# S5 coefficient generators moved from GpSimd to VectorE, and one sum and one scan per group pair in the S5 mixer

## The chip, the core and the metric

The kernel runs on one core of one Trainium2 chip. The metric is the device time of one execution in microseconds (us). In the text and in the profile the engines are PE (TensorE matmul), PEld (TensorE weight load), DVE (VectorE), ACT (ScalarE), POOL (GpSimd) and SP (SyncE, which here only issues DMAs). All data are fp32; large matmuls run on fp32r halves (a rounded high part and the rest), three matmuls for each product.

## What is computed

A network of two layers on 1024 latent tokens and 256 context tokens of width 1024. Layer 0 mixes with attention and retention, layer 1 with an S5 state space model; each is followed by an MLP of width 4096 with squared ReLU. The change touches the S5 part, whose coefficients depend on the inputs and are made on the chip:

```python
def s5_discretize(a_re, a_im, b_re, b_im, c_re, c_im, log_dt):
    a = lax.complex(f(a_re), f(a_im))
    dt = jnp.exp(f(log_dt))[:, None]
    a_bar = jnp.exp(dt * a)
    b_bar = ((a_bar - 1) / a)[..., None] * lax.complex(f(b_re), f(b_im))
    c_mat = lax.complex(f(c_re), f(c_im))
...
    # per step, 64 groups of 64 states and 16 channels, both directions
    bu = jnp.einsum('btgh,gph->btgp', u_blk.astype(jnp.complex64), b_bar)
    bu = bu.at[:, 0].add(a_bar * x)
    _, xs = lax.associative_scan(_affine_compose, (a, bu), axis=1)
    y = jnp.einsum('btgp,ghp->btgh', xs, c_mat).real
...
    z = jax.nn.gelu(y).astype(dtype) @ w_glu
    za, zb = jnp.split(z, 2, axis=-1)
    return za * jax.nn.sigmoid(zb)
```

## The kernel before

The program is written in a tile framework that allocates buffers, sets all semaphores, and orders the instructions of each engine by its own planning, in which code position is a priority; the order on an engine can therefore differ from the order in the code. Once built, each engine's queue and each DMA queue runs strictly in order.

**Layer 0's MLP** (`mlp`, called twice in `run`) first handles tokens 0 to 511 and the context, then tokens 512 to 1023. Sixteen rounds each make 256 hidden columns (`first`) and multiply the round before by the second matrix (`second`). Each 512 KB weight tile `mraw` is loaded on SP's queue and split by `split` into `uh`/`ul` or `dh`/`dl` (L76 on ACT, L84 on DVE); the hidden activations are made by a ReLU (L1053) and squares on ACT and a subtraction `al` on POOL (L84); results are added to `x` by DVE (L1070), which frees the PSUM bank.

**Under this MLP runs a generator of side work** (`side` in `run`). `beat` advances it by one step for every 1/RA (first call) or 1/RB (second call) matmuls of 512 columns. Its steps are the modulation of layer 1 (`ada_rest`), then `s5_gen`: `s5_base` (discretisation and powers of the poles; `pb`, `bb`), `s5_outputs` (the coefficients `oc` of the output side, stored to `cst`, with the lag matrices `s5_lags`), `s5_inputs` (the coefficients `wo` of the input side, 16 parts of two halves, stored to `bst` by ACT's queue) and `s5_tables` (sines and cosines, stored to `csd`), and at last layer 1's first normalisation (`s5_in`). `later(n, f)` puts `f` off by `n` steps. Complex products are made as two products and a sum; before the change most products run on POOL and the sums on DVE.

**The mixer** (`s5_main`) works on 32 pairs of groups. `load(q)` fetches the coefficients `B`, `C`, `Tt` and the table `CS` (three buffers), `spread(q)` completes `CS` on ACT. `states(q)` multiplies the inputs `ut` (L1503), rotates by `CS` (L1511), adds (L1512), scans along 160 columns with the decay `R8` (L1516, one scan for each direction and part) and rotates back to `sy` (L1519, two of three on POOL). `outs(q)` multiplies by `C` (L1537), and every fourth pair a GELU writes `Y`. In the code, `outs(q - 2)` follows `states(q)`.

**The GLU** (`glu`) transposes `Y`, splits it into `yh` and `yl`, and for each half of the tokens runs eight output columns of two 24-matmul products; `next(side, None)` advances a second generator, 24 steps of modulation for layer 1's MLP, each of four loads `aw` and four reductions (L216). Then comes layer 1's MLP.

`atile` hands out 32 shared tiles of 512 columns (and 16 of 256) to most of these parts.

Of the kernel before, what the change touches and what calls it, by code (L numbers as in the profile page):

```python
# [9 lines left out]
F32 = mybir.dt.float32  # L10
# [14 lines left out]
MAGIC = 12582912.0  # L25
NW = 14
RA = 0.07
RB = 0.125
BLOCKS = ((0, 512), (512, 512), (1024, 256))


# [20 lines left out]
class Net:  # L52
# [1091 lines left out]
    def s5_base(self):  # L1144
# [120 lines left out]
        for d in range(2):  # L1265
            o, w = self.atile(name="pb"), self.atile(name="pbw")
            o4, w4 = (x.rearrange("p (s r q) -> p s r q", s=8, r=2) for x in (o, w))
            e = slice(0, 8) if d == 0 else slice(7, None, -1)
            bc = lambda K: K[:, d::2].unsqueeze(1).to_broadcast([P, 8, 32])
            for r in range(2):  # L1270
                tt(o4[:, :, r], pr[:, e, d::2], bc((kr, ki)[r]), ALU.mult)
                nc.gpsimd.tensor_tensor(w4[:, :, r], pi[:, e, d::2], bc((ki, kr)[r]), ALU.mult)

            def add(o4=o4, w4=w4):
                tt(o4[:, :, 0], o4[:, :, 0], w4[:, :, 0], ALU.subtract)
                tt(o4[:, :, 1], o4[:, :, 1], w4[:, :, 1], ALU.add)
            self.later(1, add)

            def turn(d=d, o=o):
                tp = self.bank()  # L1280
                for k4 in range(4):
                    nc.tensor.transpose(tp[:, k4 * P:(k4 + 1) * P], o[:, k4 * P:(k4 + 1) * P], self.ident)
                st = self.atile(name="pbs")
                nc.scalar.activation(st, tp, AF.Copy)
                nc.sync.dma_start(bass.AP(tensor=self.pbd.tensor, offset=self.pbd.offset + d * 65536,
                                          ap=[[P, P], [16384, 4], [1, P]]), st.rearrange("j (k n) -> j k n", k=4))
            self.later(20, turn)
            yield

        for d in range(2):  # L1290
            x, o, t = ([self.atile(name=nm) for _ in range(2)] for nm in ("b", "bb", "bt"))
            self.bb += [o]
            for r in range(2):
                nc.scalar.dma_start(x[r], I["s5b"][r, :, d])
            kb = lambda K: K[:, d::2].unsqueeze(2).to_broadcast([P, 32, 16])
            g3 = lambda x: x.rearrange("p (g h) -> p g h", h=16)
            for r in range(2):
                tt(g3(o[r]), g3(x[r]), kb(kr), ALU.mult)
                nc.gpsimd.tensor_tensor(g3(t[r]), g3(x[1 - r]), kb(ki), ALU.mult)

            def add(d=d, o=o, t=t):
                tt(o[0], o[0], t[0], ALU.subtract)
                tt(o[1], o[1], t[1], ALU.add)
                for r in range(2):
                    v.tensor_copy(self.bx[:, d, r, 0:16], o[r][:, 496:512])
            self.later(1, add)
            yield

    def s5_tables(self):

# [31 lines left out]
    def s5_inputs(self):  # L1342

        nc, I = self.nc, self.I
        parts = [(d, g0) for d in range(2) for g0 in range(0, 64, 8)]

        def fetch(d, g0):
            b, w = ([self.atile(name=nm) for _ in range(2)] for nm in ("wb", "ww"))
            for r in range(2):
                nc.sync.dma_start(b[r], bass.AP(  # L1350
                    tensor=I["s5bt"].tensor, offset=I["s5bt"].offset + (d * 2 + r) * 4096 + g0 * 64,
                    ap=[[0, 8], [16384, 16], [1, 512]]))
                nc.sync.dma_start(w[r], bass.AP(
                    tensor=self.pbd.tensor, offset=self.pbd.offset + (d * 16 + r) * 4096 + g0 * 64,
                    ap=[[8192, 8], [0, 16], [1, 512]]))
            return b, w
        gpv = lambda x: x.rearrange("p (q n) -> p q n", n=P)
        nx = fetch(*parts[0])
        for _ in range(4):
            yield  # L1360
        for k, (d, g0) in enumerate(parts):
            b, w = nx
            if k + 1 < len(parts):
                nx = fetch(*parts[k + 1])
            qs = slice(g0 // 2, g0 // 2 + 4)
            for r in range(2):
                x, t = (self.atile(name="wo") for _ in range(2))
                nc.gpsimd.tensor_tensor(x, w[0], b[r], ALU.mult)
                yield
                nc.gpsimd.tensor_tensor(t, w[1], b[1 - r], ALU.mult)  # L1370
                self.later(2, lambda r=r, x=x, t=t: nc.vector.tensor_tensor(
                    x, x, t, ALU.add if r else ALU.subtract))
                self.later(5, lambda qs=qs, d=d, r=r, x=x: nc.scalar.dma_start(self.bst[:, qs, d, r], gpv(x)))
                yield
                yield

    def s5_outputs(self, gp):
# [6 lines left out]
        for it in range(16):  # L1384
# [6 lines left out]
            for d in range(2):  # L1391
# [6 lines left out]
                xb = [a.unsqueeze(2).to_broadcast([P, 2, 9, 16]) for a in x]  # L1398
                v9 = lambda t: t[:, :288].rearrange("p (q k h) -> p q k h", q=2, k=9)
                a, b, e, f = (self.atile(name="oc") for _ in range(4))  # L1400
                gp_tt = nc.gpsimd.tensor_tensor
                gp_tt(v9(a), xb[0], w[0], ALU.mult)
                gp_tt(v9(b), xb[1], w[1], ALU.mult)
                gp_tt(v9(e), xb[0], w[1], ALU.mult)
                gp_tt(v9(f), xb[1], w[0], ALU.mult)

                def join(a=a, b=b, e=e, f=f):
                    v.tensor_tensor(a[:, :288], a[:, :288], b[:, :288], ALU.subtract)
                    v.scalar_tensor_tensor(e[:, :288], e[:, :288], -1.0, f[:, :288], op0=ALU.mult, op1=ALU.subtract)
                self.later(2, join)  # L1410

                def store(qs=qs, d=d, a=a, e=e, k0=k0):
                    for r, t in enumerate((a, e)):
                        nc.scalar.dma_start(self.cst[:, qs, d, r], t[:, :288].rearrange("p (q k) -> p q k", q=2)[
                            :, :, 16 * k0:16 * k0 + P])
                self.later(5, store)
                o1[d] = [t[:, :288].rearrange("p (q k) -> p q k", q=2) for t in (a, e)]
                yield
            self.later(6, lambda it=it, o1=o1: self.s5_lags(it, o1))
            yield  # L1420

    def s5_lags(self, it, o1):
# [41 lines left out]
    def s5_main(self, p, last):  # L1464
# [1 line left out]
        nc = self.nc  # L1466
        v, gp, mm = nc.vector, nc.gpsimd, nc.tensor.matmul

        def inputs(g0, n):

            for s in range(8):
                nc.sync.dma_start(ut[112 - 16 * s:128 - 16 * s, g0:g0 + n],
                                  self.ud[16 * g0:16 * (g0 + n), s].rearrange("(g q) c -> q g c", q=16))
        self.Y = {(kt, th): self.atile(name="y") for kt in range(KT) for th in range(2)}
        sl, A, ybank = {}, {}, {}
# [18 lines left out]
            nc.scalar.activation(CS[:, :, 1], CS[:, :, 2], AF.Copy)  # L1494

        def states(q):
            B, C, Tt, CS = sl[q]
            for d in range(2):
                vb = self.bank()
                for r in range(2):  # L1500
                    for k in range(2):
                        u = ut[:, 2 * q + k, 0:160] if d == 0 else ut[:, 2 * q + k, 32:192]
                        mm(vb[64 * k:64 * k + 64, 160 * r:160 * r + 160], B[:, d, r, 64 * k:64 * k + 64], u,  # L1503
                           start=True, stop=True)
                t = p.tile([P, 640], F32, tag="st", name="st", bufs=2)
                t4 = t.rearrange("p (r w c) -> p r w c", r=2, w=2)
                vv = vb[:, 0:320].rearrange("p (r c) -> p r c", r=2)
                if d == 1:
                    vv = vv[:, :, ::-1]
                cs = CS[:, d].rearrange("p (r w) c -> p r w c", r=2)  # L1510
                v.tensor_tensor(t4, vv.unsqueeze(2).to_broadcast([P, 2, 2, 160]), cs[:, ::-1], ALU.mult)  # L1511
                v.tensor_tensor(t[:, 0:320], t[:, 0:320], t[:, 320:640], ALU.add)  # L1512
                z = p.tile([P, 320], F32, tag="sz", name="sz", bufs=3).rearrange("p (r c) -> p r c", r=2)
                a8 = self.R8[:, 2 * q + d:2 * q + d + 1].to_broadcast([P, 160])
                for r in range(2):
                    v.tensor_tensor_scan(z[:, r], a8, t[:, 160 * r:160 * r + 160], 0.0, ALU.mult, ALU.add)  # L1516
                y = p.tile([P, 512], F32, tag="sy", name="sy", bufs=6).rearrange("p (r w c) -> p r w c", r=2, w=2)
                e = gp if (2 * q + d) % 3 else v
                e.tensor_tensor(y if d == 0 else y[:, :, :, ::-1],  # L1519
                                z[:, :, 31:159].unsqueeze(2).to_broadcast([P, 2, 2, P]), cs[:, :, ::-1, 31:159],  # L1520
                                ALU.mult)
                A[q, d] = y

# [21 lines left out]
        for q in range(3):  # L1545
            load(q)
        ut = p.tile([P, 64, 192], F32, name="ut")
        for _ in range(3):
            next(last)
        inputs(0, 8)  # L1550
        self.drain(last)
        for q in range(32):
            spread(q)
# [10 lines left out]
    def glu(self, p, x, after, side):  # L1564
# [3 lines left out]
        for th in range(2):  # L1568
# [9 lines left out]
            for oc in range(KT):  # L1578
                b = []
                for w in (oc + KT, oc):  # L1580
                    wt = self.split(p, I["glu"][w], "u")
                    z = self.bank()
                    for kt in range(KT):
                        self.mm3(z, wt(kt), yT[kt], kt == 0, kt == KT - 1)
                        if kt % 4 == 3:
                            next(side, None)
                    b.append(z)
                sgm = p.tile([P, 512], F32, tag="r", name="sgm", bufs=2)
# [271 lines left out]
```

## Time and profile before

| what | us |
|---|---|
| median of three runs | 3227.12 (3220.26 to 3232.1) |
| the profiled execution | 3215.43 |
| its span, first to last instruction | 3213.6 |
| layer 0's MLP with the side work, in the profile | 1075 to 2081 |
| the mixer's loop over pairs, in the profile | 2102 to 2284 |

The profile is that of one execution. The page gives each engine's busy time over the whole span; a table of stretches gives the same for any part of it, with the TensorE clock that was granted (1.00 is full speed) and the share of time that the 16 DMA engines were busy. A list of waits says for how long an engine stood before a line and what ended it; a view by tile gives least, median and longest duration of each operation on that tile; a view by time lists instructions with start and duration, and in brackets the idle time before.

### The profile page before, as it was taken

The page shows a single profiled execution, that of the slowest core. Times are in us where ns is not written, and L with a number is a line of the kernel's source. Part 1 is how long each engine was busy: PE and PEld are TensorE (multiplying, and loading weights), DVE is VectorE, ACT ScalarE, POOL GpSimd, SP SyncE. Part 2 cuts the span into 40 slices and gives each one's busy share as a digit, 9 for nine tenths or more (in the row PEclk, how much of TensorE's full clock was granted, in tenths as well). Part 3 has the DMA queues.
Part 4 walks back from the last instruction along what each step waited for, and adds up shares of the span by engine and source line. Part 5 has one row for each costly group of instructions (what it writes and reads, how often), then busy time and mean ns, then how long its engine had stood idle before and what let it go on. Part 6 is the DMA issues. An engine that isn't in the chain of part 4 may idle for free. (4 is left out here: it accounts for less than half of the span.)

```text
span 3213.6 us, 45368 instructions
## 1 busy us (share of the span) xinstructions
PE 2968.0 (92%) x16683; PEld 2436.2 (76%) x16683; DVE 2111.0 (66%) x4014; ACT 1221.5 (38%) x2493; POOL 929.7 (29%) x902
## 2 busy tenths in 40 slices
PE   5899998899999998999997999967799999999998
PEld 3777777678878787887785778756678788888887
DVE  6777777687754688556468974378865555555555
ACT  6542222666762332222233664321334322222221
POOL 3642222455540113466326110123222111111111
PEclk8999999999999999999998999979999999999999
DMA  7132222301021452245426555287742111111111
GB/s 250 69 119 84 76 79 63 84 26 25 13 85 34 136 162 89 87 120 154 131 85 206 172 163 145 85 180 196 231 139 89 56 46 53 53 46 47 46 46 66
DMA packets 259039, 324.28 MB, mean 101 GB/s; under 512 B 72336, under 2 KB 179632, under 8 KB 258816
## 3 DMA queue, kind: packets, MB, share of 16 engines
q1 hardware_dynamic: 198352, 281.03, 29.0%
q10 hardware_dynamic: 59264, 36.84, 3.7%
q0 software_dynamic: 1200, 3.51, 0.4%
q8 instruction: 131, 2.15, 0.3%
q14 instruction: 92, 0.75, 0.1%
HBM read 267.96 MB, written 53.35 MB: 100 GB/s over the span
## 5 line engine op out<-in xcount | busy, mean ns | idle before, releaser
L84 POOL TENSOR_TENSOR al<-r,ah 128x512 fp32r<-128x512 f32 (+1 forms) x160 | 204.3, 1289 | 1191.5 <-ACT r L1057 1116.7
L1070 DVE SCALAR_TENSOR_TENSOR x<-b,mods,x 128x512 f32<-128x512 f32 (+1 forms) x483 | 457.5, 967 | 101.1 <-PE b L72 95.1
L84 DVE TENSOR_TENSOR ul<-mraw,uh 128x512 fp32r<-128x512 f32 x256 | 204.6, 803 | 429.3 <-ACT uh L76 428.7
L70 PE MATMUL b<-ah,dh 128*128 128x512 f32 (+1 forms) x1088 | 416.1, 383 | 21.4 <-ACT r L1053 10.2
L71 PE MATMUL b<-al,dh 128*128 128x512 f32 (+1 forms) x1088 | 413.7, 380 | 0.7 <-POOL al L84 0.7
L72 PE MATMUL b<-ah,dl 128*128 128x512 f32 (+1 forms) x1088 | 412.7, 380 | 0.5 <-DVE dl L84 0.4
L76 ACT ACTIVATE uh<-mraw 128x512 fp32r<-128x512 f32 x256 | 160.3, 628 | 453.3 <-PE b L71 261.3
L70 PE MATMUL b<-h2h,uh 128*128 128x512 f32 (+1 forms) x768 | 280.7, 366 | 21.8 <-DVE x L1070 11.6
L72 PE MATMUL b<-h2h,ul 128*128 128x512 f32 (+1 forms) x768 | 278.9, 364 | 18.6 <-DVE ul L84 18.4
L71 PE MATMUL b<-h2l,uh 128*128 128x512 f32 (+1 forms) x768 | 277.5, 361 | 0.0
L70 PEld LDWEIGHTS b<-ah,dh 128*128 128x128 f32 x1088 | 206.7, 190 | 64.8 <-DVE x L1070 11.6
L72 PEld LDWEIGHTS b<-ah,dl 128*128 128x128 f32 x1088 | 206.5, 190 | 40.5 <-DVE dl L84 1.9
L71 PEld LDWEIGHTS b<-al,dh 128*128 128x128 f32 x1088 | 207.0, 190 | 38.1 <-POOL al L84 1.1
L76 ACT ACTIVATE dh<-mraw 128x512 fp32r<-128x512 f32 x192 | 117.5, 627 | 248.2 <-PE b L71 119.6
L84 POOL TENSOR_TENSOR pl<-pe,ph 128x512 fp32r<-128x512 f32 (+1 forms) x128 | 158.3, 1246 | 154.9 <-ACT ph L76 86.8
L70 PE MATMUL b<-h3h,uh 128*128 128x512 f32 x512 | 202.0, 395 | 0.0
L71 PE MATMUL b<-h3l,uh 128*128 128x512 f32 x512 | 200.0, 391 | 2.0 <-DVE h3l L313 1.8
L72 PE MATMUL b<-h3h,ul 128*128 128x512 f32 x512 | 200.9, 393 | 0.0
L70 PEld LDWEIGHTS b<-h2h,uh 128*128 128x128 f32 x768 | 146.6, 191 | 50.5 <-DVE x L1070 14.2
L84 DVE TENSOR_TENSOR dl<-mraw,dh 128x512 fp32r<-128x512 f32 x192 | 150.5, 794 | 48.5 <-ACT dh L76 28.9
L72 PEld LDWEIGHTS b<-h2h,ul 128*128 128x128 f32 x768 | 146.4, 191 | 47.1 <-DVE ul L84 23.7
L1053 ACT ACTIVATE r<-b 128x512 f32<-128x512 f32 (+1 forms) x160 | 87.9, 550 | 244.9 <-PE b L72 170.8
(421 smaller groups left out, 7171.3 us busy)
## 6 DMA issues: line engine op xcount, KB each, us to landing
mraw<-in_w SPq DMA_DIRECT2D x192, 512.0 KB
aw<-in_adat SPq DMA_DIRECT2D x112, 256.0 KB
mraw<-in_glu SPq DMA_DIRECT2D x32, 512.0 KB
aw<-in_adat SPq DMA_DIRECT2D x96, 128.0 KB
CS<-csd SPq DMA_DIRECT2D x32, 320.0 KB
w<-in_adaw SPq DMA_DIRECT2D x32, 256.0 KB
wraw<-in_winr SPq DMA_DIRECT2D x32, 256.0 KB
cst<-oc ACTq DMA_DIRECT2D x64, 128.0 KB
```

The costliest lines, as they stand in the source:

```text
L70: mm(o, s[0], m[0], start=start, stop=False)
L71: mm(o, s[0], m[1], start=False, stop=False)
L72: mm(o, s[1], m[0], start=False, stop=stop)
L76: self.nc.scalar.activation(o, x, AF.Copy)
L84: e.tensor_tensor(o, x, h.bitcast(F32), ALU.subtract)
L1053: nc.scalar.activation(r[:, :n], b[:, :n], AF.Relu)
L1070: nc.vector.scalar_tensor_tensor(o, as_x(b), self.M[:, l, 5, oc, s:s + 1], xs, op0=ALU.mult, op1=ALU.add)
```

## The change

RB goes from 0.125 to 0.14. In `s5_base`, `s5_outputs` and `s5_inputs` all products move to DVE, each sum follows its products at once instead of one or two steps later, and `s5_base` and `s5_outputs` are divided into more steps (22 and 32 more). In `states` the two directions' rotated inputs go into one tile; one addition of 640 columns makes the sums of both directions and parts, and one scan of 640 columns runs over all four; for it, a tile `dec` holds the decay in every column but the first of each stretch of 160, where it is zero, made by ACT from a mask. `sy` comes from the shared tiles. The first eight loads of `ut` alternate between ACT's queue and SP's. In `glu` the second generator isn't advanced in the very first output column.

```diff
-RB = 0.125
+RB = 0.14
...
             for r in range(2):
                 tt(o4[:, :, r], pr[:, e, d::2], bc((kr, ki)[r]), ALU.mult)
-                nc.gpsimd.tensor_tensor(w4[:, :, r], pi[:, e, d::2], bc((ki, kr)[r]), ALU.mult)
...
+                yield
+                tt(w4[:, :, r], pi[:, e, d::2], bc((ki, kr)[r]), ALU.mult)
+                tt(o4[:, :, r], o4[:, :, r], w4[:, :, r], (ALU.subtract, ALU.add)[r])
+                yield
...
+            yield
+            yield
             for r in range(2):
                 tt(g3(o[r]), g3(x[r]), kb(kr), ALU.mult)
-                nc.gpsimd.tensor_tensor(g3(t[r]), g3(x[1 - r]), kb(ki), ALU.mult)
...
+                yield
+                tt(g3(t[r]), g3(x[1 - r]), kb(ki), ALU.mult)
+                yield
+                tt(o[r], o[r], t[r], (ALU.subtract, ALU.add)[r])
+                v.tensor_copy(self.bx[:, d, r, 0:16], o[r][:, 496:512])
+                yield
...
-                nc.gpsimd.tensor_tensor(x, w[0], b[r], ALU.mult)
+                nc.vector.tensor_tensor(x, w[0], b[r], ALU.mult)
                 yield
-                nc.gpsimd.tensor_tensor(t, w[1], b[1 - r], ALU.mult)
-                self.later(2, lambda r=r, x=x, t=t: nc.vector.tensor_tensor(
-                    x, x, t, ALU.add if r else ALU.subtract))
-                self.later(5, lambda qs=qs, d=d, r=r, x=x: nc.scalar.dma_start(self.bst[:, qs, d, r], gpv(x)))
+                nc.vector.tensor_tensor(t, w[1], b[1 - r], ALU.mult)
                 yield
+                nc.vector.tensor_tensor(x, x, t, ALU.add if r else ALU.subtract)
+                self.later(3, lambda qs=qs, d=d, r=r, x=x: nc.scalar.dma_start(self.bst[:, qs, d, r], gpv(x)))
                 yield
...
-                gp_tt(v9(a), xb[0], w[0], ALU.mult)
-                gp_tt(v9(b), xb[1], w[1], ALU.mult)
-                gp_tt(v9(e), xb[0], w[1], ALU.mult)
-                gp_tt(v9(f), xb[1], w[0], ALU.mult)
...
+                v.tensor_tensor(v9(a), xb[0], w[0], ALU.mult)
+                v.tensor_tensor(v9(b), xb[1], w[1], ALU.mult)
+                v.tensor_tensor(a[:, :288], a[:, :288], b[:, :288], ALU.subtract)
+                yield
+                v.tensor_tensor(v9(e), xb[0], w[1], ALU.mult)
+                v.tensor_tensor(v9(f), xb[1], w[0], ALU.mult)
+                v.scalar_tensor_tensor(e[:, :288], e[:, :288], -1.0, f[:, :288], op0=ALU.mult, op1=ALU.subtract)
...
-                self.later(5, store)
+                self.later(3, store)
...
-            self.later(6, lambda it=it, o1=o1: self.s5_lags(it, o1))
+            self.later(4, lambda it=it, o1=o1: self.s5_lags(it, o1))
...
+            dec = p.tile([P, 2, 2, 160], F32, tag="dec", name="dec", bufs=2)
+            for d in range(2):
+                nc.scalar.activation(dec[:, d], mask, AF.Copy, scale=self.R8[:, 2 * q + d:2 * q + d + 1])
+            t = p.tile([P, 2, 2, 320], F32, tag="st", name="st", bufs=1)
...
-                v.tensor_tensor(t4, vv.unsqueeze(2).to_broadcast([P, 2, 2, 160]), cs[:, ::-1], ALU.mult)
-                v.tensor_tensor(t[:, 0:320], t[:, 0:320], t[:, 320:640], ALU.add)
...
-                for r in range(2):
-                    v.tensor_tensor_scan(z[:, r], a8, t[:, 160 * r:160 * r + 160], 0.0, ALU.mult, ALU.add)
-                y = p.tile([P, 512], F32, tag="sy", name="sy", bufs=6).rearrange("p (r w c) -> p r w c", r=2, w=2)
+                v.tensor_tensor(t[:, d].rearrange("p r (w c) -> p r w c", w=2),
+                                vv.unsqueeze(2).to_broadcast([P, 2, 2, 160]), cs[:, ::-1], ALU.mult)
+            sm = p.tile([P, 2, 320], F32, tag="sm", name="sm", bufs=1)
+            v.tensor_tensor(sm, t[:, :, 0], t[:, :, 1], ALU.add)
+            z = p.tile([P, 2, 2, 160], F32, tag="sz", name="sz", bufs=2)
+            v.tensor_tensor_scan(z.rearrange("p d r c -> p (d r c)"), dec.rearrange("p d r c -> p (d r c)"),
+                                 sm.rearrange("p d c -> p (d c)"), 0.0, ALU.mult, ALU.add)
+            for d in range(2):
+                cs = CS[:, d].rearrange("p (r w) c -> p r w c", r=2)
+                y = self.atile(name="sy").rearrange("p (r w c) -> p r w c", r=2, w=2)
...
+        mask = p.tile([P, 2, 160], F32, name="mask")
+        v.memset(mask, 1.0)
+        v.memset(mask[:, :, 0:1], 0.0)
...
-        inputs(0, 8)
+        inputs(0, 8, (nc.scalar, nc.sync))
...
-                        if kt % 4 == 3:
+                        if kt % 4 == 3 and (th or oc):
                             next(side, None)
```

More of the change, by code (lines that the diff above doesn't have):

```diff
@@ L1271, in s5_base @@
                 tt(o4[:, :, r], pr[:, e, d::2], bc((kr, ki)[r]), ALU.mult)
-                nc.gpsimd.tensor_tensor(w4[:, :, r], pi[:, e, d::2], bc((ki, kr)[r]), ALU.mult)
[L1274 to L1277, printed above, removed]
+                yield
+                tt(w4[:, :, r], pi[:, e, d::2], bc((ki, kr)[r]), ALU.mult)
+                tt(o4[:, :, r], o4[:, :, r], w4[:, :, r], (ALU.subtract, ALU.add)[r])
+                yield
             def turn(d=d, o=o):
@@ L1296, in s5_base @@
             g3 = lambda x: x.rearrange("p (g h) -> p g h", h=16)
+            yield
+            yield
             for r in range(2):
                 tt(g3(o[r]), g3(x[r]), kb(kr), ALU.mult)
-                nc.gpsimd.tensor_tensor(g3(t[r]), g3(x[1 - r]), kb(ki), ALU.mult)
-            def add(d=d, o=o, t=t):
-                tt(o[0], o[0], t[0], ALU.subtract)
-                tt(o[1], o[1], t[1], ALU.add)
-                for r in range(2):
-                    v.tensor_copy(self.bx[:, d, r, 0:16], o[r][:, 496:512])
-            self.later(1, add)
-            yield
+                yield
[4 more added lines that the diff above has]
+                yield
     def s5_tables(self):
@@ L1400, in s5_outputs @@
                 a, b, e, f = (self.atile(name="oc") for _ in range(4))
-                gp_tt = nc.gpsimd.tensor_tensor
-                gp_tt(v9(a), xb[0], w[0], ALU.mult)
-                gp_tt(v9(b), xb[1], w[1], ALU.mult)
-                gp_tt(v9(e), xb[0], w[1], ALU.mult)
-                gp_tt(v9(f), xb[1], w[0], ALU.mult)
[L1407 to L1410, printed above, removed]
+                v.tensor_tensor(v9(a), xb[0], w[0], ALU.mult)
[5 more added lines that the diff above has]
+                v.scalar_tensor_tensor(e[:, :288], e[:, :288], -1.0, f[:, :288], op0=ALU.mult, op1=ALU.subtract)
                 def store(qs=qs, d=d, a=a, e=e, k0=k0):
@@ L1467, in s5_main, with inputs @@
         v, gp, mm = nc.vector, nc.gpsimd, nc.tensor.matmul
-        def inputs(g0, n):
+        def inputs(g0, n, engs=(nc.sync,)):
             for s in range(8):
-                nc.sync.dma_start(ut[112 - 16 * s:128 - 16 * s, g0:g0 + n],
+                engs[s % len(engs)].dma_start(ut[112 - 16 * s:128 - 16 * s, g0:g0 + n],
                                   self.ud[16 * g0:16 * (g0 + n), s].rearrange("(g q) c -> q g c", q=16))
@@ L1504, in states @@
                            start=True, stop=True)
-                t = p.tile([P, 640], F32, tag="st", name="st", bufs=2)
-                t4 = t.rearrange("p (r w c) -> p r w c", r=2, w=2)
                 vv = vb[:, 0:320].rearrange("p (r c) -> p r c", r=2)
@@ L1510, in states @@
                 cs = CS[:, d].rearrange("p (r w) c -> p r w c", r=2)
[L1511 to L1516, printed above, removed]
-                y = p.tile([P, 512], F32, tag="sy", name="sy", bufs=6).rearrange("p (r w c) -> p r w c", r=2, w=2)
+                v.tensor_tensor(t[:, d].rearrange("p r (w c) -> p r w c", w=2),
[8 more added lines that the diff above has]
+                y = self.atile(name="sy").rearrange("p (r w c) -> p r w c", r=2, w=2)
                 e = gp if (2 * q + d) % 3 else v
                 e.tensor_tensor(y if d == 0 else y[:, :, :, ::-1],
-                                z[:, :, 31:159].unsqueeze(2).to_broadcast([P, 2, 2, P]), cs[:, :, ::-1, 31:159],
+                                z[:, d, :, 31:159].unsqueeze(2).to_broadcast([P, 2, 2, P]), cs[:, :, ::-1, 31:159],
                                 ALU.mult)
```

## The prediction

> **What bounds the kernel now.** I read the page's totals first, then busy time by stage, then the waits of the stages that fall short.
>
> ```profile
> span 3213.6 us, 45368 instructions
> PE 2968.0 (92%) x16683; PEld 2436.2 (76%) x16683; DVE 2111.0 (66%) x4014; ACT 1221.5 (38%) x2493; POOL 929.7 (29%) x902
> PE   5899998899999998999997999967799999999998
> ```
>
> TensorE is busy 92% of the span, so a gain can only come from the slices below 9. The table by stage (start:end, length, then busy time and count for PE, PEld, DVE, ACT, POOL; granted clock, DMA share, GB/s) covers layer 0's MLP, under which the S5 coefficients are generated, then the S5 mixer and the GLU's start:
>
> ```profile
> 1200.00:1260.00 60.00, 50.85 (x281) 43.56 (x280) 57.63 (x178) 16.15 (x33) 21.68 (x20) 0.94 0.27 85
> 1320.00:1500.00 180.00, 172.76 (x1347) 144.38 (x1346) 99.89 (x163) 51.56 (x121) 104.08 (x129) 1.00 0.41 121
> 1500.00:1560.00 60.00, 47.60 (x270) 40.16 (x269) 38.95 (x39) 11.84 (x25) 43.19 (x30) 0.89 0.65 207
> 1560.00:1640.00 80.00, 80.00 (x463) 70.41 (x462) 34.17 (x45) 25.96 (x52) 11.22 (x11) 1.00 0.22 67
> 1690.00:1750.00 60.00, 40.71 (x149) 30.61 (x148) 44.30 (x41) 15.53 (x29) 48.18 (x32) 0.79 0.68 211
> 1750.00:1880.00 130.00, 126.94 (x544) 101.96 (x543) 126.32 (x311) 83.22 (x146) 16.90 (x13) 0.99 0.59 178
> 1880.00:2080.00 200.00, 198.03 (x865) 161.71 (x865) 95.09 (x143) 90.79 (x149) 27.17 (x22) 0.99 0.44 126
> 1960.00:2060.00 100.00, 100.00 (x435) 81.34 (x434) 39.30 (x55) 38.22 (x62) 11.64 (x9) 1.00 0.39 119
> 2104.00:2281.00 177.00, 137.13 (x2616) 113.06 (x2612) 150.09 (x277) 35.60 (x92) 58.45 (x46) 0.93 0.79 199
> 2281.00:2299.00 18.00, 5.29 (x91) 4.85 (x92) 15.72 (x62) 4.19 (x9) 1.43 (x1) 0.77 0.67 222
> 2299.00:2350.00 51.00, 49.11 (x203) 38.64 (x202) 45.41 (x132) 20.79 (x33) 8.77 (x5) 0.95 0.70 221
> ```
>
> Two rows give the undisturbed pace: 463 matmuls in 80 us (5.79 per us, where 256- and 512-wide ones alternate) and 435 in 100 us (4.35 per us, all 512 wide, in the MLP's second call). Against them, 1200-1260 does 281 instead of 347 and loses 11.4 us; 1500-1560 does 270 instead of 347 and loses 13.3 us; 1690-1750 does 149 instead of 261 and loses 25.7 us, more than its 19.3 us of idle PE, since the granted clock falls to 0.79. The tables' stage (1750-1880) does 544 instead of 566, 5 us. The lost stages are those where POOL is most busy. The waits of 1500-1560 and then of 1690-1750 (total, times, longest) say why:
>
> ```profile
> ACT uh L76 <- DMA mraw<-in_w: 18.0, 2, 10.1
> DVE wo L1371 <- POOL wo L1370: 9.2, 6, 2.5
> PE b L70 <- ACT r L1053: 6.3, 1, 6.3
> ...
> ACT r L1053 <- DVE wo L1371: 11.4, 2, 5.7
> PE b L70 <- DVE x L1070: 8.5, 1, 8.5
> PE b L72 <- DVE ul L84: 7.5, 2, 6.7
> ```
>
> This is a chain through in-order queues: POOL makes the two products of `wo`, DVE stands at the sum until POOL is done, ACT stands at the store of `wo` (L1373) until the sum is there, and behind these stand the MLP's own weight splits, ReLUs and bank evictions, for which PE waits. A second cause stands in the first row: the weights (`mraw`) land late.
>
> **The input coefficients (L1368-1373).** 64 products leave POOL for DVE.
>
> ```profile
> L1368 POOL TENSOR_TENSOR wo<-ww,wb x32: 1252/1466/1766, 1501.5 to 1747.1; 128x512 f32<-128x512 f32 x32
> L1370 POOL TENSOR_TENSOR wo<-ww,wb x32: 1264/1708/1748, 1502.7 to 1748.8; 128x512 f32<-128x512 f32 x32
> L1371 DVE TENSOR_TENSOR wo<-wo x32: 675/1334/1782, 1508.8 to 1751.6; 128x512 f32<-128x512 f32 x32
> ```
>
> (Least, median and longest ns.) The sum takes 675 ns when POOL is idle and 1334 in the median: the two engines slow each other. One part now costs POOL about 3.2 us and DVE 1.3 us; after, DVE alone 3 x 0.68 = 2.0 us with no cross-engine wait.
>
> Of the 39.0 us lost in the two stages I take back 26, two thirds: the `wo` chain goes, but the late `mraw` stays, 18.0 of the 60.9 us of the six waits listed. Bounds: 39, all of it, and 5, if the weights' landing was what ended last anyway. The 32 stores stay, two steps earlier. Note where the steps fall: a step is one advance of the generator. The MLP's first call has (2304 - 51) x 0.07 = 157 steps. Before, 41 of modulation, 19 of base and 48 of outputs leave 49 of the 100 input steps to it; after, base has 41 and outputs 80, so all 100 input steps lie in the second call, at 1 / 0.14 / 4.35 = 1.64 us each. There DVE has 32 x 2.0 = 65 us for inputs, 126.3 - 0.393 x 130 = 75 us for tables, 95.1 - 0.393 x 200 = 17 for the last normalisations, and 0.393 x 353 = 139 for the MLP: 296 of the 353 us that 1536 matmuls take. It fits. The generator needs 324 steps and gets 157 + 215 = 372, so nothing is left to drain.
>
> **Base and output coefficients.**
>
> ```profile
> L1271 DVE TENSOR_TENSOR pb<-pw,gc x4: 420/1122/1299, 1237.1 to 1245.2; 128x256 f32<-128x256 f32 x4
> L1298 DVE TENSOR_TENSOR bb<-b,gc x4: 679/685/1557, 1249.0 to 1254.3; 128x512 f32<-128x512 f32 x4
> L1403 POOL TENSOR_TENSOR oc<-c,pw x32: 697/710/1164, 1255.5 to 1478.2; 128x288 f32<-128x288 f32 x32
> L1408 DVE TENSOR_TENSOR oc<-oc x32: 444/939/1554, 1257.8 to 1479.4; 128x288 f32<-128x288 f32 x32
> ```
>
> In base, 12 DVE operations of about 0.42 and 12 of 0.68 take 13 us, spread over 26 steps; now the same sums run beside POOL at up to three times their least. But 1200-1260 is mostly a run of small DVE operations that stay (DVE 57.6 of 60 us). I take 4 of the 11.4 us; bounds 0 and 8. In the outputs 128 POOL products of some 0.8 us become DVE products of 0.44: 56 us more on an engine that is 55% busy there (99.9 of 180), partly given back by sums at 444 instead of 939. PE idles 7.2 us in that stage; I take 3, bounds -3 and 5.
>
> **The mixer's sums and scans.**
>
> ```profile
> L1237 DVE TENSOR_TENSOR gc<-pw x7: 208/211/214, 1221.8 to 1233.2; 128x64 f32<-128x64 f32 x7
> L1519 DVE TENSOR_TENSOR sy<-sz,CS x22: 659/682/1585, 2107.1 to 2282.6; 128x512 f32<-128x512 f32 x22
> L1516 DVE TENSOR_TENSOR_SCAN sz<-R,st x128: 456/465/1498, 2105.9 to 2280.9; 128x160 f32<-128x160 f32 x128
> ...
> 2129.00 1.53 DVE L1511 TENSOR_TENSOR st<-b,CS 128x640 f32<-128x640 f32 x2
> 2130.45 0.93 DVE L1512 TENSOR_TENSOR st<-st 128x320 f32<-128x320 f32 x2
> 2131.30 1.62 DVE L1516 TENSOR_TENSOR_SCAN sz<-R,st 128x160 f32<-128x160 f32 x4
> ...
> 2124.58 1.56 DVE L1511 TENSOR_TENSOR st<-b,CS 128x640 f32<-128x640 f32 x2 [5.71 <-ACT CS L1494]
> ```
>
> DVE works 150.1 of 177 us here. No row has a scan of 640. From 64 and 512 columns a two-input operation costs (659 - 208) / 448 = 1.01 ns per column and 0.14 us fixed; with the same fixed part a scan of 160 costs (456 - 143) / 160 = 1.96 ns per column, so 640 take 1.40 us against 1.62 for the four that now follow each other. Nearest bounds: 0.95 us (the further columns at 1.01 ns) and 1.86 (four times 465 ns). The sum of 640 columns takes 0.79 against 0.93. That is 0.36 us per pair; but product, sum, scan and product now each need the one just before, where two directions used to interleave, about 0.1 us for each of two to three. The net is near nothing: I take 2 us over the 32 pairs. Bounds: 20 (cheap scan) and -10 (POOL's and PE's share of a pair starts only after the longer scan). The 27 us in which DVE stands here, in pieces like the last row's 5.71 us for `CS`, end with a load that can go out only when an earlier pair's `CS` is free; they hardly move. `sy` leaves six buffers of its own for the shared 512-column tiles; its slots come free with the same matmuls, so I cost that at nothing (at worst it is in the -10). The masked factors add two 128x320 activations per pair to ACT, busy 35.6 of 177 us, which hides them; uncovered they would cost some 0.9 us per pair.
>
> [...]
>
> **Start of the mixer, start of the GLU.**
>
> ```profile
> 2093.40 3.93 SPq L1472 DMA_DIRECT2D ut<-ud  x8
> ...
> 2270.95 21.32 SPq L212 DMA_DIRECT2D aw<-in_adat  x29
> 2292.32 1.37 SPq L1004 DMA_DIRECT2D mraw<-in_glu  x3
> ...
> 2288.12 0.47 DVE L216 CUSTOM_DVE_ANT_0 aw<-aw,silr,mods 128x256 f32<-128x256 f32 x1
> ...
> 2288.53 0.47 DVE L216 CUSTOM_DVE_ANT_0 aw<-aw,silr,mods 128x256 f32<-128x256 f32 x1
> ...
> 2298.48 1.97 PE L1573 MATMUL b<-ident,y 128*128 128x128 f32 x8 [11.22 <-DVE yl L84]
> ```
>
> Eight first loads on two queues save half of 3.93 us: 2 (bounds 0 and 2; ACT's following activations stand behind its four). At the GLU, PE waits 11.2 us because DVE first works off modulation reductions, 0.41 us apart, of which 29 loads went out ahead of the GLU's own. The code asks for 16 of them in the first output column and 13 in the second, so the order already reaches a column ahead. Without the first column's 16 I take 16 x 0.41 = 6 us; bounds 0 (others move up) and 11. The 16 land in later columns, where DVE has 5.6 us to spare in 51 and PE runs at 203 matmuls in 51 us.
>
> **The sum.** 26 + 4 + 3 + 2 + 2 + 6 = 43 us. The profiled execution took 3215.4 us (span 3213.6 and 1.8 around it), 11.7 below the median 3227.1; from the execution it gives 3172, and on the median's basis 3184, which I forecast.
>
> **Rivals.** *More than that:* all 39 us of the inputs, 8, 5, 11 of the GLU and a cheap scan at 20 with 2 make 85: 3142. For it speaks that lost time counts extra through the clock (0.79); against it the scan's 1.96 ns per column. *The weights' landing was the last wait:* inputs give nothing, the GLU's reductions move up again, and 4 + 3 + 2 + 2 = 11 remain: 3216. For it the 18.0 us on `mraw` and 211 GB/s; against it that PE's own waits name ACT and DVE. *DVE becomes the bound in the second call, the slower end:* at 0.14 the tables' 44 steps pass in 72 us of PE time and need 75 + 28 us of DVE, 31 us too much, times 25.7 / 19.3 for the clock = 41 us; and with DVE full, splits wait as now, so the inputs' 26 are not won: 41 - 17 = +24, 3251. It decides as soon as the tables cannot start before their steps are due. Against it: in 1750-1880 DVE is already at 126 of 130 us and PE loses only 5.
>
> **Chances.** Forecast 0.52, more 0.13, late weights 0.23, DVE bound 0.12. A measurement of this kernel can tell 0.5%, 16 us: faster means below 3211, slower above 3243. Nearly all of the first case, the second and a little of the third are faster: 0.68; same 0.20; slower 0.12. The likeliest case alone spans 3160 to 3207. The range is 3150 to 3232: it leaves out the DVE case and half of the high gain.
>
> **What would show it.** Right: no `wo`, `oc`, `pbw` on POOL, sums at their least time, PE near 4.35 per us through the inputs; one scan per pair near 1.4 us and about 150 us of DVE in the mixer as before; the wait for `yl` near 5 us. Wrong: PE waiting for `x` or `ul` with DVE at 95% or more in the MLP's second call; ACT waiting long for `mraw`; a scan near 0.95 us; a mixer much longer or shorter than 177 us.

## The result and the profile after

The changed kernel takes 3198.22 us (median of four runs, 3195.11 to 3202.96) against 3224.27 for the kernel before in the same series: ratio 0.9922, 95% interval 0.9903 to 0.9942, some 25 us less. The forecast was 3184, with a range of 3150 to 3232. The profiled execution took 3195.87 us against 3215.43. Executions of one kernel lie up to some 20 us apart and a profile shows one of them, so small differences between two profiles mean little.

The page of the changed kernel, its totals and the slices that answer to those of before:

```profile
span 3193.8 us, 45085 instructions
PE 2964.4 (93%) x16683; PEld 2441.1 (76%) x16683; DVE 2137.4 (67%) x4088; ACT 1255.4 (39%) x2559; POOL 732.7 (23%) x702
PE   5899998899999999999998898968899999999998
```

POOL has lost 197 us of work, DVE has gained only 26. Its own operations beside POOL's became faster (the sums of `wo` take 686 ns in the median, 1334 before), and the mixer's scans went from 128 of 465 ns to 32 of 1492, some 12 us less.

```profile
L1369 DVE TENSOR_TENSOR wo<-wo x32: 679/686/1781, 1671.1 to 1834.2; 128x512 f32<-128x512 f32 x32
```

TensorE still has weak slices, but later ones. The table by stage says which (columns as before: start:end, length, busy time and count for PE, PEld, DVE, ACT, POOL; clock, DMA share, GB/s):

```profile
1200.00:1260.00 60.00, 55.75 (x302) 47.58 (x302) 55.92 (x186) 18.04 (x38) 9.62 (x8) 0.97 0.28 84
1320.00:1500.00 180.00, 180.00 (x1213) 156.84 (x1212) 109.55 (x203) 56.89 (x120) 26.73 (x21) 1.00 0.31 93
1660.00:1840.00 180.00, 151.76 (x643) 121.08 (x642) 123.36 (x194) 56.21 (x97) 17.82 (x14) 0.91 0.72 216
1910.00:2010.00 100.00, 83.75 (x341) 66.25 (x340) 71.63 (x165) 60.19 (x105) 9.45 (x7) 0.91 0.63 166
```

Base and outputs run as hoped: in 1320-1500 PE never stands (before, it stood 7.2 us). With more steps the outputs now last from 1360 to 1657, where they lasted from 1255 to 1480, so only half of them fall into that stretch. The inputs now lie in 1660-1840, and there TensorE does 643 matmuls where 4.35 per us would make 783: 32.2 us lost, nearly the 39.0 of before. In 1910-2010, where the last tables and normalisations run, it does 341 instead of 435: 21.6 us lost, in a stage that lost hardly anything before (865 of 870 in 1880-2080).

Where the gain sits can be read off two more rows for each kernel: the scans of the mixer in the view by tile (least, median and longest ns, first and last start) and, in the view by time, the first column that the GLU adds to `x`. After:

```profile
L1512 DVE TENSOR_TENSOR_SCAN sz<-dec,sm x32: 1484/1492/1495, 2096.8 to 2261.3; 128x640 f32<-128x640 f32 x32
```
```profile
2293.86 2.13 POOL L1594 TENSOR_TENSOR x<-x,sgm 128x512 f32<-128x512 f32 x1 [29.57 <-DVE sgm L1592]
```

and before (its scans are quoted in the prediction, 2105.9 to 2280.9):

```profile
2314.59 2.08 POOL L1592 TENSOR_TENSOR x<-x,sgm 128x512 f32<-128x512 f32 x1 [32.16 <-DVE sgm L1590]
```

Up to the first scan 9.1 us are gained, in the scans' loop 10.5 (175.0 to 164.5), from the last scan to the GLU's first column 1.1. That is all of the 20.7 us by which the first column comes earlier; behind it 0.9 us go back, to 19.8 in the span.

So three things were to be explained: why the inputs gave so little, why the tables' end became costly, and why the mixer gave five times its term.

### The profile page after: what moved, and what is told of

It is laid out like the page before. It is cut to its first block, busy times and chain, and to the rows that moved or that the text cites. A ratio compares the mean times of both kernels' runs of the same rounds, so it can differ in the third digit from the quotient of the medians.

```text
span 3193.8 us, 45085 instructions
## 1 busy us (share of the span) xinstructions
PE 2964.4 (93%) x16683; PEld 2441.1 (76%) x16683; DVE 2137.4 (67%) x4088; ACT 1255.4 (39%) x2559; POOL 732.7 (23%) x702
## 3 DMA queue, kind: packets, MB, share of 16 engines
q1 hardware_dynamic: 197776, 280.63, 29.2%
## 5 line engine op out<-in xcount | busy, mean ns | idle before, releaser
L1070 DVE SCALAR_TENSOR_TENSOR x<-b,mods,x 128x512 f32<-128x512 f32 (+1 forms) x483 | 460.5, 965 | 105.2 <-PE b L72 99.9
L84 DVE TENSOR_TENSOR ul<-mraw,uh 128x512 fp32r<-128x512 f32 x256 | 194.7, 767 | 394.6 <-ACT uh L76 394.2
L70 PE MATMUL b<-h2h,uh 128*128 128x512 f32 (+1 forms) x768 | 284.8, 371 | 42.8 <-DVE x L1070 30.0
L70 PE MATMUL z<-wh,hh 128*128 128x512 f32 (+1 forms) x400 | 161.6, 404 | 11.8 <-ACT scr L497 6.2
```

The source lines that it names most:

```text
L70: mm(o, s[0], m[0], start=start, stop=False)
L84: e.tensor_tensor(o, x, h.bitcast(F32), ALU.subtract)
L1070: nc.vector.scalar_tensor_tensor(o, as_x(b), self.M[:, l, 5, oc, s:s + 1], xs, op0=ALU.mult, op1=ALU.add)
```

## The parts alone

**Generators.** The kernel before with the new `s5_base`, `s5_outputs`, `s5_inputs` and RB = 0.14, and nothing else.

> The kernel before with the coefficient generators of the change alone (base, outputs and inputs on VectorE, the new steps, RB 0.14); mixer, first ut loads and GLU as before. Theory A (the forecast's terms: the POOL-to-DVE chain was what stopped TensorE in the inputs stage): 26 + 4 + 3 = 33 us less than before, ratio 0.990, and layer 0's MLP ends some 33 us earlier. Theory B (read off the trace of after: TensorE stops in that stage for late weights and for ACT standing at the stores of wo, and the stops only move later): about 8 us less, the 7.6 us by which layer 0's MLP ends earlier in the trace of after, ratio 0.9975; the stage of the inputs still loses over 30 us of TensorE.

Measured: 3202.82 us, ratio 0.9947 (0.9926 to 0.9968), 17 us. The inputs' stage loses what it loses in the whole change:

```profile
1660.00:1840.00 180.00, 155.40 (x651) 123.62 (x650) 126.00 (x205) 57.00 (x100) 18.45 (x14) 0.92 0.72 217
1910.00:2010.00 100.00, 86.97 (x347) 68.76 (x346) 70.17 (x157) 58.99 (x103) 9.51 (x7) 0.90 0.63 165
```

132 matmuls short in the first stretch, 30 us. Theory A is out; B understated the time (8 us), but the stage is as it said.

**The same with the inputs' products left on GpSimd.**

```diff
-                nc.vector.tensor_tensor(x, w[0], b[r], ALU.mult)
+                nc.gpsimd.tensor_tensor(x, w[0], b[r], ALU.mult)
```

(and the second product, the sum and the store as in the kernel before.)

> As the run with the generators alone, but the 64 products of the inputs stay on GpSimd, with their sums and stores as before; base and outputs on VectorE, RB 0.14. Theory A: the inputs' 26 us are missing, 7 us less than before, so 26 us slower than the run with the generators alone. Theory B: base and outputs carry the gain and the inputs' products hardly matter: within 6 us of the run with the generators alone.

Measured: 3212.13 us, ratio 0.9973 (0.9956 to 0.9991). The inputs' products are worth 0.0026 of the time, 8 us, where the forecast had 26; the two intervals overlap, so it may be less. Theory A, 26 us slower, is out; theory B, at most 6, is passed by a little.

```profile
1660.00:1840.00 180.00, 138.37 (x598) 108.87 (x597) 126.71 (x163) 57.27 (x100) 112.36 (x76) 0.87 0.69 219
```

The stage does 598 matmuls instead of 651, 12 us of difference by the pace of 4.35; with or without POOL's products 30 to 43 us are lost there, and 217 to 219 GB/s move.

**The mixer.** The kernel before with `dec`, `sm`, one scan for each pair, and `sy` from the shared tiles.

> The kernel before with the merged sums and scans of the mixer alone (masked factors, one sum and one scan per pair, sy in the shared tiles); generators, first ut loads and GLU as before. Theory A (the forecast's term): 2 us less than before. Theory B (the trace of after, where the mixer's loop went from 181.7 to 174 us): 8 us less, ratio 0.9975. If the loop's gain in after came from the order of what reaches the mixer and not from the merging: 0.

Measured: 3212.80 us, ratio 0.9969 (0.9956 to 0.9983), 10 us; its scans run from 2112.0 to 2276.5, 164.5 us as in the whole change. The part by itself brings all of the mixer's gain.

**First loads of `ut` and the GLU's guard**, the kernel before with these two alone.

> The kernel before with the first ut loads on two queues and without modulation steps in the GLU's first output column; generators and mixer's sums as before. Theory A (the forecast's terms): 2 + 6 = 8 us less. Theory B (the trace of after: 2.3 us at the mixer's start, and some 13 us between the last GELU and the GLU's first column, since the wait for yl is gone altogether): 13 to 15 us less, ratio 0.9955.

Measured: 3213.92 us, ratio 0.9985 (0.9970 to 1.0000): hardly anything. SP's queue at the GLU shows why the guard does nothing:

```profile
2268.47 21.24 SPq L212 DMA_DIRECT2D aw<-in_adat  x29
2289.76 1.37 SPq L1004 DMA_DIRECT2D mraw<-in_glu  x3
```

There are 29 loads ahead of the GLU's weights with the guard, as without it (2270.95 in the prediction's rows): as we read it, the planner hoists later columns' loads into the place of those that were taken out, since their tiles are free.

The three parts' gains sum to 0.0099, the whole change has 0.0078; within the intervals, no gain or loss of their combination is shown.

## What stops TensorE under the inputs

Four runs start from the changed kernel. **The factors loaded once:** only the first of 16 parts loads `wb` and `ww`, all parts use these, so 60 loads of 256 KB are left out.

```diff
-            if k + 1 < len(parts):
-                nx = fetch(*parts[k + 1])
```

> The changed kernel, but the inputs' factors wb and ww are loaded for the first of the 16 parts only and used for all: 60 loads of 256 KB (15.7 MB) are left out, all products, sums and stores stay. Before the change the 1660-1840 stretch is to be compared with: in after 38.8 MB moved there at 216 GB/s and TensorE lost about 38 us against its steady pace. Theory C (the transfers are the limit of that stage: factors, stores and the MLP's weights together want more than the 216 GB/s that come): TensorE's loss in the stage falls under 12 us, the kernel is 20 to 30 us faster than after, ratio to before 0.984. Theory D (ACT's queue, in which the stores stand until wo is there, is the limit): at most 8 us faster. Theory E (VectorE's added operations are the limit): no change.

**One product:** each half is one product instead of two and a sum, so 64 DVE operations are left out, with all loads and stores kept.

```diff
-                nc.vector.tensor_tensor(x, w[0], b[r], ALU.mult)
+                nc.vector.tensor_tensor(x, w[r], b[r], ALU.mult)
                 yield
-                nc.vector.tensor_tensor(t, w[1], b[1 - r], ALU.mult)
                 yield
-                nc.vector.tensor_tensor(x, x, t, ALU.add if r else ALU.subtract)
```

> The changed kernel, but each of the inputs' 32 halves is made by one product instead of two products and their sum: 64 VectorE operations of 0.68 us (43 us) are left out, all loads and stores stay. Theory C (transfers): at most 6 us faster than after. Theory D (ACT stands at the stores until wo is there): the stores' data are ready two steps earlier and ACT no longer stands there, 15 us or more faster. Theory E (VectorE): 20 us or more faster, ratio to before 0.985.

**The stores on GpSimd's queue:** `nc.gpsimd.dma_start(self.bst...)` for `nc.scalar.dma_start`.

> The changed kernel, but the 32 stores of wo are issued from GpSimd's queue instead of ACT's. In after ACT stands some 48 us in 1660-1840 until wo is there. Theory D (that standing delays the weight splits and ReLUs for which TensorE waits): 15 to 30 us faster than after. Theory C (transfers): within 5 us of after, ACT then stands longer for the weights mraw instead. Theory E: no change.

Measured: 3153.68 us for the factors loaded once, ratio 0.9812 (0.9798 to 0.9827), 35 us faster than the change; 3200.03 for one product, 0.9956 (0.9942 to 0.9970), not faster; 3195.97 for the stores, 0.9948 (0.9930 to 0.9967), not faster. The stage in this order, one kernel to a fence:

```profile
1660.00:1840.00 180.00, 175.65 (x779) 141.44 (x778) 178.03 (x347) 87.52 (x153) 51.16 (x17) 0.99 0.58 177
```
```profile
1660.00:1840.00 180.00, 140.50 (x610) 111.22 (x609) 102.48 (x192) 61.30 (x108) 16.69 (x12) 0.88 0.70 226
```
```profile
1660.00:1840.00 180.00, 148.12 (x619) 117.99 (x618) 125.24 (x197) 55.50 (x97) 42.33 (x45) 0.91 0.66 212
```

With the loads gone TensorE makes 779 of 783, with DVE at 99% of the stretch: DVE's work was never what stopped it (theory E is out). With a third of that work left and all loads kept, it makes 610, fewer than the change: DVE, with less to do, now stands 43.0 us for the factors' loads, where the two such waits of the changed kernel make 19.8.

```profile
DVE wo L1365 <- DMA ww<-pbd: 43.0, 18, 6.4
```

With ACT freed from the stores it makes 619 (theory D is out); ACT then stands elsewhere, as the waits of the changed kernel and of that run in this stretch show:

```profile
ACT uh L76 <- DMA mraw<-in_w: 38.2, 7, 11.8
ACT dh L76 <- DVE wo L1369: 15.1, 4, 5.1
ACT r L1053 <- DVE wo L1369: 12.9, 3, 4.3
ACT uh L76 <- DVE wo L1369: 11.2, 3, 4.0
```
```profile
ACT uh L76 <- DMA mraw<-in_w: 62.4, 7, 12.7
```

The waits for `wo` turn into waits for the MLP's weights. With the factors loaded once, that row reads 11.2 us in all.

TensorE itself has only one kind of wait in this stretch of the changed kernel, for DVE's additions to `x` (L1070), which free a PSUM bank. Its row, and two rows of what DVE stood for:

```profile
PE b L70 <- DVE x L1070: 28.2, 5, 7.5
DVE ul L84 <- ACT uh L76: 31.6, 13, 6.7
DVE wo L1367 <- DMA ww<-pbd: 13.0, 5, 3.1
```

The 28.2 us are all the time that TensorE is idle there. DVE's additions stand behind two things in its queue: the low halves `ul`, which wait for ACT's splits and so for late weights, and the products of `wo`, which wait for late factors (13.0 us at the second product and 6.8 at the first). In the other runs TensorE's wait goes with the sum of the two: 31.9 us with the stores on GpSimd's queue (42.8 for `ul`, 11.2 for the factors), 33.0 with one product (31.1 and 43.0), 4.3 with the factors loaded once (0.9 and none). So it is the factors' loads that hold this stage, by two paths: they make the MLP's weights late, and they are late themselves. Leaving them out takes away their bytes and their places in SP's queue at once; these runs do not part the two.

## The step rate

**The change with RB = 0.125**, as it was before.

> The changed kernel with RB 0.125 as before instead of 0.14: the 100 input steps in the MLP's second call come 1.84 us apart instead of 1.64 and take 184 us instead of 164. Theory C (transfers): the same bytes over a longer time, 16.8 + 8.4 MB over 184 us leave 20 GB/s more to the weights; 6 to 12 us faster than after. Theory D and E: 3 to 8 us faster. If later steps make the last tables and normalisations collide with the end of the MLP instead: 0 to 10 us slower.

Measured: 3169.94 us, ratio 0.9860 (0.9845 to 0.9875): 20 us faster than the change, more than any theory gave.

```profile
1660.00:1840.00 180.00, 157.33 (x671) 125.54 (x670) 128.94 (x210) 59.94 (x105) 19.90 (x14) 0.94 0.71 221
1910.00:2010.00 100.00, 97.76 (x434) 79.04 (x433) 75.58 (x162) 64.83 (x115) 12.42 (x9) 1.00 0.61 160
```

The inputs' stage gains 28 matmuls, 6 us: it moves 221 GB/s as before, for the planner hoists the products, of which the first of each half lie within 153 us here (1669.4 to 1822.1) and 160 in the change (1668.7 to 1828.9), so that the rate of steps hardly spreads them. The end of the tables gains 93 matmuls, 21 us. In the change the stretch begins with a full DVE and goes on at a low clock:

```profile
1910.00:1930.00 20.00, 18.48 (x81) 14.82 (x80) 19.76 (x55) 12.16 (x22) 2.71 (x2) 1.00 0.57 183
1930.00:1950.00 20.00, 16.85 (x71) 12.83 (x70) 19.90 (x51) 13.53 (x25) 2.90 (x2) 1.00 0.59 186
1950.00:1970.00 20.00, 17.18 (x70) 13.70 (x70) 13.68 (x29) 12.71 (x21) 0.00 (x0) 0.83 0.44 131
1970.00:1990.00 20.00, 14.87 (x61) 12.08 (x60) 12.81 (x25) 15.76 (x30) 2.56 (x2) 0.83 0.71 134
```

With RB = 0.125 DVE is as full in 1910-1950, but PE makes 172 matmuls there instead of 152, and the clock stays at 1.00 to 2010. That the rate costs this kernel 20 us is shown. It is not the rate alone, though: with the inputs' products on GpSimd and with one product, both at 0.14, the same stretch has 417 and 414 matmuls. The tables' first operation starts at 1817.9 and 1802.4 us there, at 1838.9 in the change and at 1829.4 with RB = 0.125, where the last one starts at 1952.6 and 1951.2: the change packs the tables into the least time. TensorE's own waits in 1910-2010 are 16.2 us in the change, 6.0 of them for ACT's `uh` and 4.5 for the normalisation's `acc` on DVE, and 2.2 with RB = 0.125. What makes these late isn't shown; the longest wait on DVE (`ul` for `uh`, 18.9 us) is 11.2 with RB = 0.125 too.

**Inputs ahead of the outputs**, so that their loads lie in the MLP's first call, with RA 0.085 and RB 0.1.

```diff
+        yield from self.s5_inputs()
         yield from self.s5_outputs(gp)
-        yield from self.s5_inputs()
```

> The changed kernel with the inputs' coefficients generated ahead of the outputs' and the steps at RA 0.085 and RB 0.1 (191 + 153 = 344 steps for 324): base and inputs then lie in the MLP's first call, in which after moves 100 GB/s beside a TensorE that never stands (1360-1600), outputs and tables in its second call. Theory C (transfers): TensorE's loss in layer 0's MLP falls from 104 us to some 65, as with the factors loaded once (58), ratio to before 0.981. If stalls in the engines' queues (sums, stores, splits) go with the inputs wherever they are: ratio 0.988 or more.

Measured: 3188.15 us, ratio 0.9887 (0.9866 to 0.9909). The stall goes with the inputs:

```profile
1331.00:1480.00 149.00, 127.57 (x682) 107.56 (x681) 100.80 (x156) 32.15 (x63) 17.79 (x12) 0.95 0.68 202
```

The first products of the halves lie within 148 us (1331.2 to 1479.5), PE stands 21 us, and 202 GB/s move. Theory C had counted on the loads being spread by the steps; they aren't.

## The mixer and the GLU

**Only `sy` in the shared tiles**, in the kernel before; 128 scans and 64 sums as they were.

```diff
-                y = p.tile([P, 512], F32, tag="sy", name="sy", bufs=6).rearrange(
+                y = self.atile(name="sy").rearrange(
```

> The kernel before with sy in the shared 512-column tiles instead of six buffers of its own, nothing else. Theory H (the mixer's 9.5 us come from the merged sums and scans): the mixer's loop stays at 175.5 us, ratio 1.000. Theory I (they come from sy's buffers, with which the next loads go out earlier): the loop is some 8 us shorter, ratio 0.9975.

Measured: 3210.27 us, ratio 0.9962 (0.9946 to 0.9978), 12 us: as much as the whole mixer part (0.9969).

```profile
L1516 DVE TENSOR_TENSOR_SCAN sz<-R,st x128: 457/468/1587, 2109.9 to 2274.2; 128x160 f32<-128x160 f32 x128
```
```profile
SPq L1481 <- DVE sy L1519: 26.4, 13, 3.9
SPq L1481 <- POOL sy L1519: 14.8, 9, 3.6
```

The loop, first to last start of the scans, is 164.3 us long with the old scans (the rows are the scans of this run and the waits of SP's queue during its loop: total, times, longest). The same waits before show what six buffers did:

```profile
SPq L1481 <- POOL sy L1519: 46.2, 11, 8.5
SPq L1481 <- DVE sy L1519: 13.1, 7, 4.7
```

The load of `CS` (L1481) waits until the two `sy` products that read an earlier `CS` are done, and behind it in SP's queue stand all other loads: 59.3 us before, 41.2 with shared tiles. In the loop 200 GB/s move before and 217 with shared tiles. That the products come earlier because they have more buffers to write to is the reading of these rows; the wait for a free `sy` buffer isn't listed by itself.

**Eight buffers of their own for `aw`**, in the changed kernel, so that the planner can't hoist more than eight loads.

```diff
+                aw = lambda: mp.tile([P, 256], F32, tag="aw", name="aw", bufs=8)
-                yield from self.ada_rest(a256, ...
+                yield from self.ada_rest(aw, ...
```

> The changed kernel, but the modulation weights aw of the GLU's stage get eight buffers of their own instead of the shared tiles. In after 22 of their loads stand ahead of the GLU's first weights in SP's queue (19.23 us), as 29 did before and in the run of mixer and GLU start, where the guard alone left all 29 there; with eight buffers of their own none stands ahead. Theory F (this queue is what holds the GLU's start): the GLU's first column is done 8 to 13 us earlier after the last scan, ratio to before 0.989. Theory G (the chain from the last scan through the last GELUs, transposes and splits takes that long anyway): at most 3 us; later columns then wait for modulation instead, or nothing changes.

Measured: 3180.83 us, ratio 0.9876 (0.9856 to 0.9897), 15 us faster than the change. The queue and the end of the GLU's first column in this run, ahead of that the queue and ACT in the change:

```profile
2250.20 19.23 SPq L212 DMA_DIRECT2D aw<-in_adat  x22
2269.53 1.32 SPq L1004 DMA_DIRECT2D mraw<-in_glu  x3
2274.58 0.63 ACT L76 ACTIVATE uh<-mraw 128x512 fp32r<-128x512 f32 x1 [17.97 <-issue]
2276.52 0.38 ACT L1541 ACTIVATE y<-z 128x256 f32<-128x256 f32 x1
```
```profile
2246.12 9.63 SPq L1004 DMA_DIRECT2D mraw<-in_glu  x3
2255.80 4.61 SPq L212 DMA_DIRECT2D aw<-in_adat  x8
2275.71 2.10 POOL L1594 TENSOR_TENSOR x<-x,sgm 128x512 f32<-128x512 f32 x1 [20.80 <-DVE sgm L1592]
```

In the change 27 loads, 22 of them in the row's window, still stand ahead of the GLU's weights; ACT stands 17.97 us at their split, and the last GELUs are queued behind it. (The profile names nothing that ACT waited for there, "issue"; that it was the weights is read from their place 5 us ahead of the split.) With none ahead, the first column comes 24.1 us after the last scan (2251.6) instead of 32.6, and the mixer's loop, in which those loads and their reductions had begun, is 158.0 us long. Theory F holds.

**All together:** RB = 0.125, eight `aw` buffers, and the factors' loads on GpSimd's queue.

> The changed kernel with RB 0.125 as before the change, eight buffers of its own for aw in the GLU's stage, and the inputs' factors wb and ww loaded from GpSimd's queue, so that the MLP's weights mraw no longer stand behind them in SP's queue. The first two alone should add up: 0.986 from the run with RB 0.125 and 0.0046 less from the eight buffers, ratio 0.9814. Theory C in its plain form (the bytes that move are the limit, whatever queue they are on): 0.981, TensorE's loss in layer 0's MLP stays near 75 us. Theory J (what counts is that the weights stand behind the factors in SP's queue): the weights land in time, the loss falls towards the 58 us of the run with the factors loaded once, ratio 0.976 or less. If GpSimd's queue is a poor one for 256 KB loads: the inputs take longer and the gain of 0.981 is partly lost.

Measured: 3146.19 us, ratio 0.9800 (0.9783 to 0.9818), faster than both kernels (the kernel before: 3214.84 beside it).

```profile
1660.00:1840.00 180.00, 164.69 (x722) 131.59 (x721) 152.56 (x266) 72.99 (x126) 57.86 (x75) 0.98 0.91 239
```

The stage loses 14 us instead of the 26 with RB = 0.125 alone, with the same bytes to move at 239 GB/s, so 216 to 221 GB/s were no ceiling. The time, however, is what theory C gave (0.981), and theory J's 0.976 or less lies outside its interval. Nor did the weights come in time, as the waits of this run in the stage show:

```profile
PE b L70 <- DVE x L1070: 15.3, 7, 4.4
ACT uh L76 <- DMA mraw<-in_w: 35.6, 7, 7.2
DVE ul L84 <- ACT uh L76: 21.1, 7, 5.7
```

ACT's wait for them is 35.6 us where it is 25.6 with RB = 0.125 alone. What fell is what DVE stands for, the splits from 29.2 us to 21.1 and the factors from 11.1 to 1.8, and TensorE's wait with it from 22.7 to 15.3. So the place of the weights behind the factors in SP's queue is not shown to cost anything. The gain of the stage itself is read from one profile each: this one took 3139.28 us where the median is 3146.19, that with RB = 0.125 took 3173.70 where it is 3169.94. How the remaining 14 us come about stays open.

## Why the forecast was right, and where it was wrong

The sign and the range were right, and 3184 is 14 us low. That the sum came this near is in part luck: the inputs gave 18 us less than their term and the GLU's start 5 less, the mixer gave 8 more, and a loss of 20 us was in no term. The same change with RB = 0.125 gains 45 us, close to the 43 forecast, but from other terms: the inputs' stage gives 13 there (39 to 26 lost) and the mixer's loop 9. One by one:

- **Inputs, 26 us.** By TensorE's count the stage lost 39.0 before and 32.2 after, 7 us of gain; the run without this part gives 8. The step that failed is "the `wo` chain goes, but the late `mraw` stays", valued at two thirds for the chain. The chain did go (`wo` sums 679/686 ns), but what is taken from it, the loads' waits take over: 31.6 us of DVE for splits whose weights are late and 19.8 for the factors. The forecast's case "the weights' landing was the last wait" was nearest to this stage, and "against it that PE's own waits name ACT and DVE" was the error: these stood for the weights and factors in their turn. That "the lost stages are those where POOL is most busy" pointed the wrong way already: POOL is busy 104 of 180 us in 1320-1500, which lost little, and 22 of 60 in 1200-1260, which lost 11.4.
- **RB, not priced.** The forecast asked whether 324 steps fit and found nothing left to drain. The raise costs 20 us. The rival "DVE becomes the bound" had the place, the tables' end with DVE at 99%, and twice the price (41 us). Its mechanism isn't shown: DVE is as full there with RB = 0.125, at no loss.
- **Base, 4 us, and outputs, 3.** 21 matmuls more in 1200-1260 make 3.6 us; in the outputs' stretch all 7.2 us of idle PE are gone. DVE has 109.6 of 180 us there and not the 156 that 99.9 and 56 make, since only half of the outputs' operations (96 of 192, 43.7 us) fall into it; the other half lies in 1500-1660.
- **Sums and scans, 2 us.** The scan of 640 columns takes 1.49 us against the 1.40 forecast. From 160 columns (465 ns) to 640 (1492) each further column costs 2.14 ns, where the prediction's rows give 1.01 for a two-input operation: no cheap scan. That the merging nets nothing was right: 164.5 us of loop with it, 164.3 without. But "its slots come free with the same matmuls, so I cost that at nothing" was wrong: `sy`'s buffers are the mixer's whole 10.5 us; that they act through SP's queue is read from its waits.
- **Start of the mixer, 2 us.** From the end of layer 0's MLP to the first scan it is 25.3 us before, 23.8 after, and 23.8 with the generators alone and one queue; with the two queues in the kernel before it is 24.5. No gain of the two queues beyond 0.8 us can be seen.
- **GLU's start, 6 us.** 1.1 came. The bound "0 (others move up)" was the case; PE's wait for `yl` went, as forecast, and came back as 7.6 us for `y`, behind a weight split on ACT.

## What to carry to other kernels

Where an engine waits for work of another, look at what both wait for before pricing the handover: here loads were late, and moving or leaving out arithmetic changed who waited. Ahead of "costs nothing", look in the DMA queue's own waits for which buffer holds up a load: here all that stood behind the load of `CS` waited with it, 59.3 us in the mixer's loop before. In a planned program, taking work out of one place in the code frees slots that the planner fills from later; a small set of buffers of its own is what holds the work back.

## What the runs showed of the hardware

- POOL and DVE slowed each other: the sum of `wo`, 128x512, takes 685 ns in the median in the run of the generators alone, and 1742 in the one in which the inputs' products are on POOL, with sums and stores put off as before; POOL's products themselves take 1.49 and 1.71 us in the median there, and 1.25 at their least.
- The granted clock was low where TensorE had idled: 0.83 in 1950-1990 of the change, with TensorE idle 4.7 us of the 40 ahead of it and 8.0 of these 40, and 1.00 in the same stretch with RB = 0.125, where it idled 0.8 and 0.9.
- Loads of 256 KB issued from GpSimd's queue were no slower for the stage than from SP's: 239 GB/s moved (all together) against 221 (RB = 0.125 alone). The DMA engines were busier for it, with a share of 0.91 against 0.71.
